# Half of the U tiles of the dense experts: 4 KB rows and PE transposes in place of 1 KB rows and DVE transposes

## The chip, the cores and the metric

The kernel runs on one core of a Trainium2 chip. The metric is the device time of one execution in microseconds; the runs shown of the kernel before took 2079.33, 2078.69 and 2074.76 us.

## What is computed

Two blocks on 512 tokens of width 1024: a pool mixer with a layer norm, then a mixer (gated convolution and RG-LRU) and a PEER layer. The change lies in PEER, where each token picks 16 of 128 x 128 = 16384 experts for each of 8 heads:

```
q = (xb @ w_q).reshape(p, PEER_HEADS, 2, PEER_DK_HALF)
sc = jnp.einsum('phcd,hcnd->phcn', q, sub_keys)
...                                     # top 16 key pairs per head: idx, softmax weights g
act  = gelu(einsum('phkd,pd->phk', expert_u[idx], xb))
out  = einsum('phk,phkd->pd', g * act, expert_v[idx])
```

`expert_u` (U) and `expert_v` (W) are 16384 x 1024 in float32.

## The kernel before

One token tile of 128 gathers its experts by index (POOL issues the indirect DMAs, DVE does a multiply with a row sum for U and a multiply-add for V). The other 384 tokens treat PEER densely: for all 16384 experts, 128 at a time ("an expert" below is such a block of 128; there are 128 of them), the scores are computed, put through gelu, multiplied by the tokens' weights (zero for experts that were not picked) and multiplied with W.

An expert i has two parts. `stage_a(i)` (line 869) brings the U block into the transposed form, splits it into `uh + ul` (float32r halves), and makes 24 score products (L138 to L140, `aux<-h2h,uh` and so on, 128x384) into a side bank of PSUM; ACT's gelu gives `gl`. `stage_v(i)` (line 922) multiplies `gl` by the weights `gt` on DVE (L931), splits the result into `wh, wl`, loads and splits the W block (`wraw`, then `whi` on ACT and `wlo` on DVE or POOL by turns), and makes 18 output products (`o<-whi,wh` and so on, 128x512) into six banks that accumulate over all experts. The loop at the end of the kernel calls `stage_a(i + 11)` and `stage_v(i)` for i = 0 to 127, with the gathers of the other token tile spread between them. The scores of the first 38 experts are made earlier, so the loop makes those of 38 to 127. Every eighth expert a 1.5 MB `gt` tile is loaded (L919).

How U gets transposed depends on a type `ty`. The loop uses type 2: `u_load` (L534) reads the block in four DMAs of 128 KB in rows of 1 KB, each into 32 partitions, and `u_turn` (L539) does 32x32 transposes on DVE from `uraw` to `ut`; ACT then copies `uh` (L112) and DVE subtracts for `ul` (L116). Ten experts before the loop use type 0: one DMA in whole rows of 4 KB (L877), eight 128x128 transposes on PE into two side banks (L881), and ACT copies out of them (L883, L887).

The raw tiles of U and W share three buffers of the tag `wraw`. All loads are issued by SP's queue in order. A scheduler orders the instructions of each engine when the kernel is built, so an engine's order is not the order of the code. In the loop two PSUM banks (`side_bank`) serve the transposes and score products.

Of the kernel before, what the change touches and what calls it, by code (L numbers as in the profile page):

```python
# [13 lines left out]
OP = mybir.AluOpType  # L14
# [10 lines left out]
NG = 1  # L25
# [53 lines left out]
def _body(tc, nc, a, outer):  # L79
# [13 lines left out]
    def banks(stack, n):  # L93
        """the banks from here on, n of them for what waits on other engines"""
        nonlocal ps, psum, naux
        psum.close()
        psum, naux = stack, n
        ps = psum.enter_context(tc.tile_pool(name="ps", bufs=1, space=PSUM, reuse_waits="tile"))
# [4 lines left out]
    def side_bank():  # L103
        """for what waits on other engines, so that it holds up no other product"""
        return ps.tile([P, 512], F32, name="aux", tag="aux", bufs=naux)

    def split(hi, lo, src, pool=False):
        """src = hi + lo exactly, each in the 12 bits that a float32r product carries"""
        if pool > 1:
            G.tensor_copy(hi, src)  # L110
        else:
            S.activation(hi, src, AF.Copy)  # L112
        if pool:
            G.tensor_tensor(lo, src, hi.bitcast(F32), op=OP.subtract)  # L114
        else:
            V.tensor_tensor(lo, src, hi.bitcast(F32), op=OP.subtract)  # L116
# [164 lines left out]
    def last_group(g, mhl, sz):  # L281
        """gates and outputs of the last group, one half of the tokens after the other"""
# [138 lines left out]
    def nrsqrt(v, scale, eps, pool=False, plus=False):  # L421
        """-1/sqrt(v*scale + eps) of one column (or its negative): an estimate, then one Newton step"""
        new = lambda nm: tiny.tile([P, 1], F32, name=nm, tag=nm)
        w, s, q, r = new("rw"), new("rs"), new("rq"), new("rr")
        S.activation(s, v, AF.Abs_reciprocal_sqrt, bias=epst[:, eps], scale=4.0 * scale)      # ~ 1/2 of the root's inverse
        (G if pool else V).tensor_scalar(w, v, 4.0 * scale, epst[:, eps], op0=OP.mult, op1=OP.add)
        if plus:
            m = new("rm")
            (G if pool else V).tensor_scalar(m, s, -1.0, None, op0=OP.mult)
        else:  # L430
            m = s
        if pool:
            G.tensor_tensor(q, s, s, op=OP.mult)
            G.tensor_tensor(q, q, w, op=OP.mult)
            G.tensor_scalar(r, q, -3.0, m, op0=OP.add, op1=OP.mult)
            return r
        V.scalar_tensor_tensor(q, s, w, s, op0=OP.mult, op1=OP.mult)
        V.scalar_tensor_tensor(r, q, -3.0, m, op0=OP.add, op1=OP.mult)
        return r

    def rms(t, xn, dve=False):
        """xn = -ya[t] / rms(ya[t])"""
        ss = tiny.tile([P, 1], F32, name="ss", tag="ss")
        S.activation(xn, ya[t], AF.Square, accum_out=ss)
        r = nrsqrt(ss, 1.0 / D, E4, NP[1])
        if dve:
            V.tensor_scalar(xn, ya[t], r, None, op0=OP.mult)
        else:
            S.activation(xn, ya[t], AF.Copy, scale=r)

    def norm_T(pool, xn, t, which, put):
        """transposes xn (tokens of tile t), modulates, and splits"""
# [18 lines left out]
    # columns of the two modulations: -g*(1+scale) and shift; the second in the order of expert products  # L471
# [59 lines left out]
    def u_load(raw, i, a0, na):  # L531
        """rows 32a+r, columns 256q+8c+k of 128 experts: partition (q, r)"""
        for q in range(4):
            nc.sync.dma_start(raw[32 * q:32 * q + 32],  # L534
                              U[i * P + a0 * 32:i * P + (a0 + na) * 32, q * 256:(q + 1) * 256].rearrange("(a r) d -> r a d", r=32))

    def u_turn(ut, raw):
        """the 32x32 transposes: partition (q, c)"""
        V.transpose(out=ut.rearrange("p k (a r) -> p a k r", r=32), in_=raw.rearrange("p a (c k) -> p a k c", k=KD))  # L539

    def pre_u(n):
        """expert tiles with the columns on the partitions, for later"""
# [15 lines left out]
    V.scalar_tensor_tensor(m4, lam, -1.0, lam, op0=OP.mult, op1=OP.min)        # -|lam|  # L558
# [3 lines left out]
    V.tensor_tensor(s4, e4, p4, op=OP.mult)                                     # s = e/(2+e)  # L562
# [7 lines left out]
    V.scalar_tensor_tensor(p4, p4, 2.0, m4, op0=OP.mult, op1=OP.add)            # softplus(-lam)  # L570
# [42 lines left out]
    def headnorm(y, dst, gname, c):  # L613
# [3 lines left out]
        def fin():  # L617
# [6 lines left out]
            V.scalar_tensor_tensor(q, q, -3.0, r, op0=OP.add, op1=OP.mult)          # -2 times the root's inverse  # L624
# [13 lines left out]
    def lru(c, br, bi, xr, ge):  # L638
# [3 lines left out]
        S.activation(r, r, AF.Tanh, scale=sp4[:, c:c + 1])              # t = tanh(-log_a / 2)  # L642
        s_, w_, q = f("s_"), f("w_"), f("q")
        V.tensor_scalar(w_, r, 1e-30, None, op0=OP.max)
        S.activation(s_, w_, AF.Abs_reciprocal_sqrt)                            # ~ 1/sqrt(t)
# [3 lines left out]
        V.tensor_tensor(s_, s_, r, op=OP.mult)                                  # -2 sqrt(t)  # L649
        S.activation(w_, r, AF.Abs_reciprocal_sqrt, bias=1.0)  # L650
        S.activation(w_, w_, AF.Square)                                         # ~ 1/(1+t)
        V.scalar_tensor_tensor(q, r, 1.0, w_, op0=OP.add, op1=OP.mult)
        V.scalar_tensor_tensor(w_, q, -2.0, w_, op0=OP.add, op1=OP.mult)        # -1/(1+t)
        V.tensor_tensor(s_, s_, w_, op=OP.mult)                                 # sqrt(1-a^2)
        V.scalar_tensor_tensor(r, r, -1.0, w_, op0=OP.add, op1=OP.mult)         # a
        V.tensor_tensor(i_, i_, xr, op=OP.mult)
        V.tensor_tensor(s_, s_, i_, op=OP.mult)                                 # u
# [35 lines left out]
    # the chunks of the product in turn, each followed by what has become ready  # L693
# [74 lines left out]
    # the tokens of the dense experts come first  # L768
# [57 lines left out]
    def qpart(w, b, j, n):  # L826
        """queries of one head for n tiles of tokens from the j-th on"""
# [41 lines left out]
    def stage_a(i):  # L869
        uh = dn.tile([P, KD, P], F32R, name="uh", tag="uh", bufs=UB)  # L870
        ul = dn.tile([P, KD, P], F32R, name="ul", tag="ul", bufs=UB)
        ty = 4 if i < NU else ATY[i % len(ATY)] if i < RT else 2
# [130 lines left out]
    def topk(t, h0, nh):  # L1003
        """the 16 best pairs of keys of heads h0..h0+nh-1, and their weights"""
# [20 lines left out]
        # ranks (a, b) of each pick, and from them the keys  # L1025
# [63 lines left out]
    def onehot2(sT, t0):  # L1089
        """[i2 = j] of 8 tokens"""  # L1090
# [12 lines left out]
    def ahead(n):  # L1103
        """the one-hots of the n-th 8 tokens"""
# [79 lines left out]
    def paced(i):  # L1184
        """not before the products of GL experts back"""
        if len(pace) > GL >= 0:
            tc.add_manual_dep(i.ins, pace[-1 - GL].ins.name, order)
# [52 lines left out]
    for t in range(NT):  # L1240
        # the columns in parts, the last ones short
# [52 lines left out]
```

## Time and profile before

| | |
|---|---|
| runs | 2074.76, 2078.69, 2079.33 us, median 2078.69 |
| span of the profiled execution | 2087.4 us, 8.7 above that median; no other time of this execution is listed |
| the loop's steady part | 1200 to 2000 us of the span |
| busiest engines over the span | PE 88%, DVE 88% |

The span is the time from the first to the last instruction of one profiled execution; durations and waits below come from it. "Busy" of PE counts overlapping matmuls once, so the pitch from one start to the next is the better measure of its work.

### The profile page before, as it was taken

How to read it: one execution, taken by the hardware profiler on the slowest of the kernel's cores; microseconds unless marked ns; L12 is line 12 of the kernel's file. 1: busy time of each engine (PE TensorE's matmuls, PEld its weight loads, DVE VectorE, ACT ScalarE, POOL GpSimd, SP SyncE). 2: the span in 40 equal slices, each digit the busy share in tenths (PEclk: the TensorE clock that was granted, in tenths of full speed). 3: DMA queues.
4: the chain of work that ended last, by engine and by line, in shares of the span. 5: the costliest groups of instructions: out<-in, count | busy, mean ns of one | idle time of the engine just before them, and what ended most of it. 6: DMA issues, size and time to landing. Idle time of an engine off the chain costs nothing.

```text
span 2087.4 us, 26487 instructions
## 1 busy us (share of the span) xinstructions
PE 1832.4 (88%) x8939; PEld 1588.0 (76%) x8939; DVE 1844.1 (88%) x3005; ACT 812.8 (39%) x1162; POOL 939.1 (45%) x599
## 2 busy tenths in 40 slices
PE   8999898878899868788989898898988988898897
PEld 6787677756698857788867787787877877787796
DVE  8999887889759999999799998898988988989956
ACT  4433333445353345778432232232232232322334
POOL 3113222342453565442356555464555545556524
PEclk9999999989999978999999999999999999999999
DMA  5545482666352324444959999999989999999932
GB/s 166 178 141 179 141 284 74 185 203 195 118 167 80 114 80 135 152 168 183 311 184 283 300 291 272 272 265 277 298 262 278 296 270 277 294 270 293 289 124 101
DMA packets 291748, 441.11 MB, mean 211 GB/s; under 512 B 24984, under 2 KB 208132, under 8 KB 288540
## 3 DMA queue, kind: packets, MB, share of 16 engines
q1 hardware_dynamic: 254748, 305.19, 48.8%
q0 software_dynamic: 36864, 134.23, 20.7%
q8 instruction: 70, 1.15, 0.2%
q14 instruction: 66, 0.54, 0.1%
HBM read 393.11 MB, written 46.23 MB: 210 GB/s over the span
## 4 chain that ended last, share of the span: by engine, by line
DVE 38%; DMA 23%; PE 15%; issue 13%; POOL 5%; SPq 2%; ACT 2%; DVEq 0%; POOLq 0%; ACTq 0%
DMA uraw<-in_expert_u 8%; DVE og L1132 8%; DMA wraw<-in_expert_v 4%; DMA gv<-in_expert_v,idx 4%; PE bank L140 3%; PE bank L139 3%; PE bank L138 3%; DVE ut L539 3%; DMA araw<-in_w_ada 2%; DVE wlo L116 2%; SPq L534 2%; POOL wlo L114 2%; DVE sw L239 2%; DVE put L539 2%; DMA praw<-in_expert_u 1%
## 5 line engine op out<-in xcount | busy, mean ns | idle before, releaser
L114 POOL TENSOR_TENSOR wlo<-wraw,whi 128x1024 fp32r<-128x1024 f32 x116 | 304.0, 2621 | 465.2 <-ACT whi L112 438.9
L140 PE MATMUL aux<-h2h,ul 128*128 128x384 f32 x1024 | 369.2, 361 | 90.2 <-DVE ul L116 78.4
L112 ACT ACTIVATE whi<-wraw 128x1024 fp32r<-128x1024 f32 x218 | 229.5, 1056 | 509.8 <-DMA wraw<-in_expert_v 375.6
L138 PE MATMUL aux<-h2h,uh 128*128 128x384 f32 x1024 | 365.1, 357 | 16.8 <-ACT uh L112 9.8
L139 PE MATMUL aux<-h2l,uh 128*128 128x384 f32 x1024 | 360.4, 352 | 0.0
L139 PE MATMUL o<-wlo,wh 128*128 128x512 f32 x756 | 298.0, 394 | 17.5 <-DVE wlo L116 12.6
L140 PE MATMUL o<-whi,wl 128*128 128x512 f32 x756 | 293.9, 392 | 0.2 <-DVE wl L116 0.2
L138 PE MATMUL o<-whi,wh 128*128 128x512 f32 x756 | 292.3, 393 | 1.4 <-ACT wh L112 1.4
L140 PEld LDWEIGHTS aux<-h2h,ul 128*128 128x128 f32 x1024 | 203.5, 199 | 110.0 <-DVE ul L116 95.9
L1180 POOL DMA_INDIRECT gv<-in_expert_v,idx x128 | 188.0, 1469 | 206.3 <-DVE acc L1203 170.1
L539 DVE STREAM_TRANSPOSE ut<-uraw 128x1024 f32<-128x1024 f32 x98 | 213.7, 2182 | 66.1 <-DMA uraw<-in_expert_u 65.6
L1180 POOL DMA_INDIRECT gu<-in_expert_u,idx x128 | 173.7, 1357 | 144.1 <-DVE junk L1192 113.8
L138 PEld LDWEIGHTS aux<-h2h,uh 128*128 128x128 f32 x1024 | 204.6, 200 | 24.8 <-ACT uh L112 12.7
L139 PEld LDWEIGHTS aux<-h2l,uh 128*128 128x128 f32 x1024 | 203.7, 199 | 3.1
L1203 DVE SCALAR_TENSOR_TENSOR acc<-gv,cf,acc 128x1024 f32<-128x1024 f32 x127 | 182.5, 1437 | 9.5 <-DMA gv<-in_expert_v,idx 9.1
L112 ACT ACTIVATE uh<-ut 128x1024 fp32r<-128x1024 f32 x98 | 103.4, 1056 | 217.9 <-DVE ut L539 208.2
L139 PEld LDWEIGHTS o<-wlo,wh 128*128 128x128 f32 x756 | 143.1, 189 | 48.4 <-DVE wlo L116 15.1
L1192 DVE SCALAR_TENSOR_TENSOR junk<-gu,hrow 128x1024 bf16<-128x1024 f32 x128 | 164.1, 1282 | 12.7 <-DMA gu<-in_expert_u,idx 12.5
L1132 DVE TENSOR_SCALAR og<-iorow,sT 128x128 f32<-128x128 f32 x384 | 173.4, 521 | 0.0
L140 PEld LDWEIGHTS o<-whi,wl 128*128 128x128 f32 x756 | 143.2, 189 | 31.0 <-DVE wl L116 0.6
L138 PEld LDWEIGHTS o<-whi,wh 128*128 128x128 f32 x756 | 142.9, 189 | 28.9 <-ACT wh L112 1.7
L1134 PE MATMUL bank<-og,o 128*128 128x128 f32 x768 | 119.2, 302 | 48.6 <-DVE og L1132 47.1
(379 smaller groups left out, 3754.3 us busy)
## 6 DMA issues: line engine op xcount, KB each, us to landing
wraw<-in_expert_v SPq DMA_DIRECT2D x128, 512.0 KB
uraw<-in_expert_u SPq DMA_DIRECT2D x392, 128.0 KB
araw<-in_w_ada SPq DMA_DIRECT2D x96, 256.0 KB
g_d<-gs SPq DMA_DIRECT2D x24, 1024.0 KB
gt<-g_d SPq DMA_DIRECT2D x15, 1536.0 KB
wraw<-in_pool_w_in SPq DMA_DIRECT2D x32, 512.0 KB
wraw<-in_w_in SPq DMA_DIRECT2D x20, 512.0 KB
praw<-in_expert_u SPq DMA_DIRECT2D x160, 64.0 KB
```

Source lines behind the costliest of these rows:

```text
L112: S.activation(hi, src, AF.Copy)
L114: G.tensor_tensor(lo, src, hi.bitcast(F32), op=OP.subtract)
L116: V.tensor_tensor(lo, src, hi.bitcast(F32), op=OP.subtract)
L138: i = PE.matmul(out, lhsT=l[0], rhs=r[0], start=first, stop=False)
L139: PE.matmul(out, lhsT=l[0], rhs=r[1], start=False, stop=False)
L140: PE.matmul(out, lhsT=l[1], rhs=r[0], start=False, stop=last)
L539: V.transpose(out=ut.rearrange("p k (a r) -> p a k r", r=32), in_=raw.rearrange("p a (c k) -> p a k c", k=KD))
L1132: V.tensor_scalar(og, iorow, sT[:, 0, tok + u:tok + u + 1], sT[:, 2, tok + u:tok + u + 1], op0=OP.is_equal, op1=OP.mult)
L1134: PE.matmul(b[:, u * P:(u + 1) * P], lhsT=o2[:, tok % 8 + u], rhs=og, start=True, stop=True)
L1180: G.indirect_dma_start(out=r, out_offset=None, in_=src, in_offset=bass.IndirectOffsetOnAxis(ap=idx[t][:, s:s + 1], axis=0))
L1192: paced(V.scalar_tensor_tensor(junk, r, 1.0, hrow[t], op0=OP.mult, op1=OP.mult, accum_out=cf[t][:, s:s + 1]))
L1203: paced(V.scalar_tensor_tensor(acc[t], r, cf[t][:, s:s + 1], acc[t], op0=OP.mult, op1=OP.add))
```

## The change

The type of the experts past 38 becomes 2 for even and 1 for odd ones. All other differences between the two files are comments.

```
-        ty = 4 if i < NU else ATY[i % len(ATY)] if i < RT else 2
+        ty = 4 if i < NU else ATY[i % len(ATY)] if i < RT else 2 - i % 2
```

Type 1 goes through code that was there, and that no expert used. It needs no `ut` tile:

```
raw = wp.tile([P, D], F32, name="uraw", tag="wraw", bufs=3)
nc.sync.dma_start(raw, U[i * P:(i + 1) * P, :])                 # L877, one DMA
for kk in range(2):
    b = side_bank()
    for k in range(4):
        PE.transpose(b[...], raw..., ident)                      # L881
    S.activation(fl(uh), b, AF.Copy)                             # L883
    V.tensor_tensor(fl(ul), b, fl(uh).bitcast(F32), op=OP.subtract)   # L885, from PSUM
```

What the scheduler makes of it, at two places. SP's queue in the loop, with what each load waits for, before: a W load (L123) waits for DVE (the transposes that read the raw U tile in its buffer), a U load (four of L534) for the split of a W tile on POOL or DVE.

```order
L123 DMA wraw<-in_expert_v 128x1024 [waits DMAHW6_49,DMAHW7_49,DMAHW0_49,DVE_49]
L534 DMA uraw<-in_expert_u 32x4x256 [waits DMAHW1_49,Pool_49]
L534 DMA uraw<-in_expert_u 32x4x256 x2
L534 DMA uraw<-in_expert_u 32x4x256 [waits DMAHW2_49]
L123 DMA wraw<-in_expert_v 128x1024 [waits DMAHW4_49,DMAHW5_49,DMAHW3_49,DVE_49]
```

The same queue after the change, over two experts:

```order
L123 DMA wraw<-in_expert_v 128x1024 [waits DMAHW3_49,PE_49]
L534 DMA uraw<-in_expert_u 32x4x256 [waits DMAHW1_49,Pool_49]
L534 DMA uraw<-in_expert_u 32x4x256 x3
L123 DMA wraw<-in_expert_v 128x1024 [waits DMAHW3_49,DVE_49]
L877 DMA uraw<-in_expert_u 128x1024 [waits DMAHW6_49,DMAHW5_49,DMAHW7_49,DMAHW4_49,DVE_49]
```

Every second U load is one DMA (L877), and every second W load waits for PE, that is for the transposes that empty its buffer. By the semaphores' values the first W row (that of an even expert) waits for the transposes of the odd tile loaded two experts before, the second W row for the split of the first one's W on DVE, the four pieces of U for a split on POOL, and L877 for DVE's transposes of the U tile in the row before. The load of gt stands between a W load and an odd tile's L877.

PE's order in the loop before: 24 score products and 18 output products in strict turn; here the end of an expert's output products and the start of the next scores.

```order
L140 MATMUL o_9645<-whi,wl 128x512
L138 MATMUL aux<-h2h,uh 128x384
L139 MATMUL aux<-h2l,uh 128x384
L140 MATMUL aux<-h2h,ul 128x384
```

After the change: the second group of four transposes stands after six output products of an expert, and the first group in front of them. The remaining 12 follow, then the 48 score products of an odd and an even expert, most often with six output products of the next expert put among them.

```order
L138 MATMUL o_9640<-whi,wh 128x512
L139 MATMUL o_9640<-wlo,wh 128x512
L140 MATMUL o_9640<-whi,wl 128x512
L138 MATMUL o_9641<-whi,wh 128x512
L881 MATMUL aux<-ident,uraw 128x128 x4
L139 MATMUL o_9641<-wlo,wh 128x512
L140 MATMUL o_9641<-whi,wl 128x512
```

What moved: the turn on PE is now by two experts, and the transposes stand among output products.

## Rows read from the trace of the kernel before

**Rows 1.** The page's first part: busy us of each engine, its share of the span of 2087.4 us, and its instructions.
```profile
PE 1832.4 (88%) x8939; PEld 1588.0 (76%) x8939; DVE 1844.1 (88%) x3005; ACT 812.8 (39%) x1162; POOL 939.1 (45%) x599
```

**Rows 2.** Busy time by engine in the loop's steady part (columns: stretch, its length, busy us and instructions of PE, PEld, DVE, ACT, POOL; granted clock; DMA share; GB/s).
```profile
1200.00:2000.00 800.00, 709.10 (x3394) 632.05 (x3393) 717.85 (x710) 236.94 (x334) 427.75 (x269) 0.96 0.96 278
```

**Rows 3.** PE's groups of instructions from 1200 to 2000 us (busy us, mean ns of one, then idle time before them and what ended it).
```profile
L140 PE MATMUL aux<-h2h,ul 128*128 128x384 f32 x645 | 232.5, 360 | 74.1 <-DVE ul L116 74.0
L138 PE MATMUL aux<-h2h,uh 128*128 128x384 f32 x646 | 228.9, 354 | 15.1 <-ACT uh L112 8.1 <-ACT gl L904 6.9
...
L139 PE MATMUL o<-wlo,wh 128*128 128x512 f32 x486 | 189.7, 390 | 1.7 <-POOL wlo L114 1.7
L138 PE MATMUL o<-whi,wh 128*128 128x512 f32 x485 | 189.5, 391 | 0.0
L140 PE MATMUL o<-whi,wl 128*128 128x512 f32 x486 | 189.3, 390 | 0.0
```

**Rows 4.** Busy time by engine in three stretches around a load of gt (columns as in rows 2).
```profile
1304.00:1340.00 36.00, 35.13 (x179) 31.83 (x178) 36.00 (x36) 11.43 (x16) 19.80 (x13) 1.00 1.07 298
1340.00:1348.00 8.00, 3.98 (x18) 2.97 (x16) 0.01 (x1) 0.00 (x0) 0.96 (x1) 0.97 1.06 241
1348.00:1356.00 8.00, 3.98 (x11) 3.47 (x12) 7.62 (x9) 2.91 (x4) 1.89 (x2) 0.50 0.64 170
```

**Rows 5.** SP's queue and DVE in order of time in the same place (start, duration, queue, line, what; in brackets idle time and releaser).
```profile
1325.70 0.39 SPq L919 DMA_DIRECT2D gt<-g_d  x1
1327.97 9.61 SPq L534 DMA_DIRECT2D uraw<-in_expert_u  x4
...
1338.94 7.66 SPq L534 DMA_DIRECT2D uraw<-in_expert_u  x4
...
1354.36 1.73 SPq L534 DMA_DIRECT2D uraw<-in_expert_u  x4
...
1348.25 2.01 DVE L539 STREAM_TRANSPOSE ut<-uraw 128x1024 f32<-128x1024 f32 x1 [8.24 <-DMA uraw<-in_expert_u]
```

**Rows 6.** DVE's transposes in the 25 us from a load of gt on: the first (from 1248 us), the second (1325 us) and the last (1894 us) of nine such stretches; in the others the idle time is 3.8 to 5.8 us.
```profile
L539 DVE STREAM_TRANSPOSE ut<-uraw 128x1024 f32<-128x1024 f32 x2 | 4.4, 2184 | 2.0 <-DMA uraw<-in_expert_u 2.0
L539 DVE STREAM_TRANSPOSE ut<-uraw 128x1024 f32<-128x1024 f32 x2 | 4.3, 2140 | 8.2 <-DMA uraw<-in_expert_u 8.2
...
L539 DVE STREAM_TRANSPOSE ut<-uraw 128x1024 f32<-128x1024 f32 x2 | 4.3, 2136 | 2.7 <-DMA uraw<-in_expert_u 2.7
```

**Rows 7.** DVE's groups for a U tile from 1200 to 2000 us.
```profile
L539 DVE STREAM_TRANSPOSE ut<-uraw 128x1024 f32<-128x1024 f32 x83 | 181.5, 2186 | 62.8 <-DMA uraw<-in_expert_u 62.3 <-issue 0.4
L116 DVE TENSOR_TENSOR ul<-ut,uh 128x1024 fp32r<-128x1024 f32 x81 | 104.9, 1295 | 1.1 <-ACT uh L112 1.1
```

**Rows 8.** PE in order of time: the first score product of an expert, the first output product after it, and the first score product of the next.
```profile
1401.78 0.34 PE L138 MATMUL aux<-h2h,uh 128*128 128x384 f32 x1
...
1406.00 0.40 PE L138 MATMUL o<-whi,wh 128*128 128x512 f32 x1
...
1410.09 0.34 PE L138 MATMUL aux<-h2h,uh 128*128 128x384 f32 x1
```

**Rows 9.** Groups over the whole span, shapes kept apart: a subtraction on DVE with a PSUM source, ACT's copy of half a U tile out of PSUM, and of a whole one from SBUF.
```profile
L116 DVE TENSOR_TENSOR sl<-bank,sh 128x512 fp32r<-128x512 f32 x16 | 10.8, 680 | 4.3 <-ACT sh L112 4.3
L883 ACT ACTIVATE uh<-aux 128x512 fp32r<-128x512 f32 x20 | 12.4, 618 | 5.0 <-PE aux L881 5.0
L112 ACT ACTIVATE uh<-ut 128x1024 fp32r<-128x1024 f32 x98 | 103.4, 1056 | 217.9 <-DVE ut L539 208.2 <-PE aux L139 4.7 <-DVE wlo L116 2.8
```

**Rows 10.** PE in order of time around the eight transposes of a type 0 tile, and the busy time of the 4 us around it (columns as in rows 2).
```profile
995.13 1.04 PE L881 MATMUL aux<-ident,uraw 128*128 128x128 f32 x8
996.14 0.44 PE L140 MATMUL aux<-h2h,ul 128*128 128x384 f32 x1
...
994.00:998.00 4.00, 4.00 (x29) 3.84 (x28) 0.00 (x0) 4.00 (x8) 2.54 (x2) 1.00 0.87 273
```

**Rows 11.** SP's issues of whole U tiles for type 0 (count, shortest, median and longest ns, first and last start).
```profile
L877 SPq DMA_DIRECT2D uraw<-in_expert_u x10: 332/333/333, 822.4 to 959.0; - x10
```

**Rows 12.** DMA in two windows of 5 us, 1260 to 1265 (mostly 1 KB packets) and 1625 to 1630 (mostly 4 KB): packets, MB, rate, and how many packets are under each size.
```profile
DMA packets 797, 1.11 MB, mean 222 GB/s; under 512 B 90, under 2 KB 662, under 8 KB 797
...
DMA packets 507, 1.85 MB, mean 371 GB/s; under 512 B 53, under 2 KB 55, under 8 KB 507
```

**Rows 13.** A load of W: SP's issue and ACT's start on it, in order of time; then the times of the split's second half on DVE and on POOL from 1400 to 1480 us (shortest, median, longest ns).
```profile
1405.15 0.35 SPq L123 DMA_DIRECT2D wraw<-in_expert_v  x1
...
1413.20 1.06 ACT L112 ACTIVATE whi<-wraw 128x1024 fp32r<-128x1024 f32 x1 [3.92 <-DMA wraw<-in_expert_v]
...
L116 DVE TENSOR_TENSOR wlo<-wraw,whi x4: 1215/1222/1229, 1407.6 to 1468.2; 128x1024 fp32r<-128x1024 f32 x4
L114 POOL TENSOR_TENSOR wlo<-wraw,whi x4: 2404/2485/3373, 1417.6 to 1472.7; 128x1024 fp32r<-128x1024 f32 x4
```

**Rows 14.** SP's queue from 1200 to 2000 us: what it waited for (us in total, times, longest).
```profile
SPq L123 <- DVE ut L539: 138.0, 61, 5.5
SPq L534 <- DVE wlo L116: 125.8, 35, 6.3
SPq L534 <- POOL wlo L114: 108.1, 29, 8.8
```

## The prediction

> **What bounds the kernel now.** I first read the page's whole-span line: PE and DVE are both busy 88% of it [rows 1], so neither alone explains the span. The change touches only the long expert loop, so I took that stretch by itself, 1200 to 2000 us [rows 2]: PE 709, DVE 718 of 800 us, DMA share 0.96. In it the products into o were issued 485 + 486 + 486 times [rows 3]; an expert has 18 of them, so 80.9 experts passed: 9.89 us each, 79.1 us for eight. Eight is the right unit, because every eighth expert a 1.5 MB gt tile is loaded.
>
> Three views then show what the 79.1 us are. *DVE.* In 36 us without a gap, 1304 to 1340, DVE is busy 36.00 us and PE 35.13 [rows 4]: between the gt loads DVE has no free time. Its work for eight experts is 718/80.9 × 8 = 71.0 us. *The gap.* In the next 8 us DVE does nothing (0.01), and 8 us later TensorE's granted clock is 0.50, its lower level of 1.2 GHz, after PE has run dry [rows 4]. The queue rows say why [rows 5]: SP issues gt at 1325.70, then the four pieces of a U tile, whose issue alone takes 9.61 us, and DVE's transpose of it starts at 1348.25 after 8.24 us of idleness that ended with that transfer. In the nine stretches of 25 us after each gt load DVE waited so for 2.0 to 8.2 us [rows 6], 41 us together, of the 62.3 us that the stage shows for this wait [rows 7]. *PE.* The products go at fixed pitch: 24 score products took 1401.78 to 1406.00, 4.22 us, the 18 output products to 1410.09, 4.09 us [rows 8]. That is 8.31 us an expert, 66.5 for eight. PE's idle time in the stage is 74.1 + 15.1 + 1.7 = 90.9 us [rows 3], or 9.0 for eight. What is left, 79.1 − 66.5 − 9.0 = 3.6, I read as lost to the clock (mean 0.96 [rows 2], and 0.04 × 79.1 is 3.2). So PE loses 12.6 of every 79.1 us, nearly all by waiting for ul and uh, which DVE and the transfers before it bring late.
>
> **The change, part by part.** From expert 39 to 127 the odd ones change: 45 tiles, over 90 experts, or 11.25 times eight with four changed tiles each. Before that point the order of instructions is the same.
>
> *DVE.* Each changed tile loses the 32x32 transposes, 2186 ns, and the subtraction of 1295 ns [rows 7]; it gains two subtractions with a PSUM source, for which the nearest row is sl<-bank at 680 ns [rows 9]. Net −2186 − 1295 + 1360 = −2121 ns, −8.5 us for eight: DVE's work falls to 62.5 and DVE stops being the fullest engine.
>
> *ACT.* Two halves of 618 ns from PSUM replace one of 1056 [rows 9]: +0.18 us on an engine busy 237 of 800 us [rows 2]. Nothing, covered by ACT's idleness; should that cover go (ACT waits in order behind whi), it is at most 0.18 × 45 = 8 us.
>
> *PE.* Eight transposes are added. The trace has ten such tiles in an earlier stage: eight took from 995.13 to the next product at 996.14, 1.01 us [rows 10]. So +4.0 for eight experts: PE's own work is 70.5 and nothing hides it when PE has no gap. The clock was 1.00 in the 4 us around them [rows 10]. The Trainium skill, "TensorE: Matmul & The Clock Gate", Part 4, gives about 275 ns for one such transpose in a kernel (for bf16) and says that transposes do not engage the clock gate; that would be 2.2 us a tile, and the sum below would come out 1.2 × 45 = 54 us later. The trace disagrees on the first, with 126 ns each, and shows no drop.
>
> *DMA.* The bytes stay, the rows grow from 1 KB to 4 KB, and four issues become one of 0.33 us [rows 11] in place of four that took between 1.73 and 9.61 us [rows 5]. In a 5 us window full of 1 KB packets the engines moved 222 GB/s, in one of 4 KB packets 371 [rows 12]. A 0.524 MB tile is then 2.36 us of all 16 engines against 1.41, so 0 (if the neighbours in those windows make the difference) to 0.95 us less per tile, 3.8 for eight. I take it as real. By the Trainium skill, "DMA: Bandwidth & Descriptors", Specifications, rows from 512 B up already reach line rate, and the term would be 0; the two windows say otherwise, though gathers run in both.
>
> *Moved waits.* SP's order keeps its alternation, but a changed tile's buffer is now freed by PE, not DVE, and W tiles wait for that (SP's order, shown with the change). PE's order changes more: two experts' score products now stand together, and the transposes in two groups of four among the output products. A late raw tile now blocks PE directly, with both kinds of products queued behind it. On the other side the tile behind gt is always an odd one, thus one of the changed: it is one transfer, and PE takes it up only after the next two experts' products have been issued, so a late landing there can be absorbed.
>
> *The sum.* PE sets the end: 70.5 plus what PE still loses. If all 12.6 stay, eight experts take 83.1, +4.0 × 11.25 = +45 us. If all go, 70.5, −8.6 × 11.25 = −97 us. Break-even is 8.6 lost. I take the odd half of the waits for uh and ul as gone: (74.0 + 8.1)/80.9 × 8 = 8.1 a group of eight, half 4.05; the clock's 3.6 falls in proportion to the 9.0 of idleness, by 1.6. Lost: 12.6 − 5.65 = 6.95; eight experts 77.4; −1.65 × 11.25 = **−18.6 us**. The profiled span of 2087.4 becomes 2069; the runs' median is 8.7 us below that span, so I forecast 2078.7 − 18.6 = **2060**.
>
> **The rivals.** *Faster by much: the gap after gt closes.* For it: the tile that DVE waits for behind gt is a changed one, and 41 of the 62.3 us of that wait lie there. If PE's loss falls to 4, eight experts take 74.5: −4.6 × 11.25 = −52 us, 2027. Against: the even tile that follows gt keeps four pieces, whose issue took 7.66 us at the same place [rows 5]. By the Trainium skill's 512 B (the same section) the tile's length would not change, and this case would fall to a third of its chance.
>
> *Slower: the raw buffers come free too late.* Three buffers carry U and W. By the built program's waits, in a pair of experts W of the even one waits for the transposes of an odd tile on PE, and W of the odd one for the split of that W: two loads in a row. From SP's issue to ACT's start a W load took 8.05 us (1405.15 to 1413.20), its split 1.06 + 1.23 on DVE or 1.06 + 2.49 on POOL [rows 13]: 10.3 + 11.6 = 21.9 us. From W's arrival PE's order needs 12.5 us to the transposes that free the buffer of the next-but-one pair (6 + 12 output products, 34 score products, 8 transposes and 6 more output products, at the pitches above). The chain spans two pairs, so a pair takes (21.9 + 12.5 + w)/2 = 17.2 + w/2, where w is waiting in SP's, ACT's, DVE's and POOL's queues; a pair now takes 19.8. It decides from w = 5.2 on. SP's waits for such buffers are long now: 138 us in 61 waits for ut, 126 in 35 for wlo on DVE, 108 in 29 on POOL [rows 14], 2 to 4 us each. With w = 9 a pair takes 21.7: +1.9 × 45 = +86, 2164. Milder, with PE's loss unchanged, it is the +45 above, 2124. Against it: loads get lighter and DVE's queue shorter.
>
> *No difference.* PE's loss falls by just the 4.0 that the transposes add: 2075 to 2083. Two runs shown agree only to 0.2%, about 4 us, which is what I count as no change.
>
> *Dearer transposes.* With the Trainium skill's 2.2 us a tile (the section on transposes above) the forecast would be 2060 + 54 = 2114; I give this 3 in 100, since the row is direct.
>
> **How the numbers follow.** My forecast (2040 to 2074) 33%, the closed gap 20%, no difference 12%, the loss unchanged or worse (2083 to 2135) 22%, the buffer chain above that 10%, dearer transposes 3%. Faster by over 0.2%: 33 + 20 = 53%; within 0.2%: 12%; slower: 22 + 10 + 3 = 35%. For the range I leave out the lower third of the closed gap and most of the buffer chain: 2005 to 2130.
>
> **What would show it.** Right: DVE's busy time in the loop about 95 us lower (45 × 2.12), no gap on DVE that ends with uraw after a gt load, PE's idle time a third to a half lower and its clock nearer 1.00, transposes at about 1 us for eight. Wrong: PE idle before the transposes or before output products with a transfer or wlo as releaser; SP's queue waiting for PE ahead of wraw; a pair of experts above 20 us; or DMA still at 0.96 with unchanged GB/s, which would say that 4 KB rows give nothing.

## The result and the profile after

The changed kernel takes **2091.53 us** (median of 20 runs, 2073.23 to 2097.61), the kernel before 2076.89 in the same sessions (20 runs, 2068.80 to 2083.63): ratio 1.0062 [1.0046, 1.0077], some 13 us slower by the ratio. The forecast was 2060, so its direction was wrong; its range held the time. The profiled execution of the changed kernel has a span of 2093.6 us against 2087.4; the one of the kernel before is longer than each of its 20 runs, so the two traces show less than the whole difference, and may show the waits before as longer than they mostly were.

Busy time from 1200 to 2000 us (columns as in [rows 2]), and that stretch's DMA in total, which for the kernel before was 120308 packets, 80094 of them under 2 KB (the same view), at a share of 0.96 [rows 2]:

```profile
1200.00:2000.00 800.00, 737.69 (x3700) 658.98 (x3699) 653.53 (x700) 241.46 (x369) 389.34 (x265) 0.97 0.85 274
...
DMA packets 101701, 219.34 MB, mean 274 GB/s; under 512 B 8352, under 2 KB 56966, under 8 KB 101651
```

DVE's busy time fell from 718 to 654 us, the DMA share from 0.96 to 0.85 with nearly the same bytes, and PE is busier by 29 us. Yet no more experts pass. PE's groups of the same stretch, which answer [rows 3] (busy us, mean ns, idle time before and what ended it):

```profile
L138 PE MATMUL aux<-h2h,uh 128*128 128x384 f32 x641 | 224.3, 350 | 39.2 <-DVE ul L885 34.2 <-ACT uh L883 4.5
L140 PE MATMUL aux<-h2h,ul 128*128 128x384 f32 x641 | 221.9, 346 | 9.3 <-DVE ul L885 9.3
...
L139 PE MATMUL o<-wlo,wh 128*128 128x512 f32 x485 | 192.3, 397 | 1.7 <-POOL wlo L114 1.6
...
L138 PE MATMUL o<-whi,wh 128*128 128x512 f32 x486 | 173.7, 410 | 3.9 <-ACT whi L112 3.9
L881 PE MATMUL aux<-ident,uraw 128*128 128x128 f32 x320 | 48.3, 277 | 8.2 <-ACT gl L904 8.1
```

485 output products of a kind passed, as before: 80.9 experts. PE's idle time is 62.3 us instead of 90.9. The waits of [rows 3] for ul from line 116 and uh from line 112 have gone altogether, for even tiles too. In their place stand waits for the changed tiles' own halves, 34.2 + 9.3 us for DVE at line 885 and 4.5 for ACT at line 883, and 8.1 us in which the transposes wait for a side bank that a gelu has not read yet. With as many experts in the same 800 us, eight still take 79.1 us, so PE loses 79.1 − 70.5 = 8.6, the prediction's break-even: 6.2 of it idle, and the other 2.4 I put down to the clock (0.97).

DVE's groups, which answer [rows 7], and the longest waits of ACT and DVE (us in total, times, longest):

```profile
L539 DVE STREAM_TRANSPOSE ut<-uraw 128x1024 f32<-128x1024 f32 x40 | 87.3, 2183 | 37.9 <-DMA uraw<-in_expert_u 37.9
L116 DVE TENSOR_TENSOR ul<-ut,uh 128x1024 fp32r<-128x1024 f32 x41 | 66.5, 1621 | 0.1
L931 DVE TENSOR_TENSOR gl<-gl,gt 128x384 f32<-128x384 f32 x80 | 60.4, 755 | 34.8 <-ACT gl L904 34.8
...
L885 DVE TENSOR_TENSOR ul<-aux,uh 128x512 fp32r<-128x512 f32 x79 | 53.7, 683 | 0.0
L116 DVE TENSOR_TENSOR wlo<-wraw,whi 128x1024 fp32r<-128x1024 f32 x41 | 50.0, 1220 | 49.3 <-ACT whi L112 49.3
```

```profile
ACT whi L112 <- DMA wraw<-in_expert_v: 213.8, 49, 11.2
ACT gl L904 <- PE aux L140: 175.7, 52, 11.9
...
DVE wlo L116 <- ACT whi L112: 49.3, 19, 5.8
```

The changed tiles' durations are those forecast: 683 ns for a half out of PSUM (680 in [rows 9]), 2183 for the transposes. An even tile's subtraction grew from 1295 ns [rows 7] to 1621, for a reason that no run here shows; that is a part of why DVE's busy time fell by 64 us and not by the 85 that 40 tiles at 2.12 make. DVE gave back its time as 84 us of waiting for ACT.

One turn shows the new wait. These rows are in order of time, first DVE's, then ACT's, then PE's (start, duration, what; in brackets idle time and its end; "..." stands for rows left out):

```profile
1328.89 0.54 DVE L931 TENSOR_TENSOR gl<-gl,gt 128x384 f32<-128x384 f32 x1
1330.86 1.23 DVE L1192 SCALAR_TENSOR_TENSOR junk<-gu,hrow 128x1024 bf16<-128x1024 f32 x1 [1.43 <-DMA gu<-in_expert_u,idx]
...
1333.25 1.28 DVE L1203 SCALAR_TENSOR_TENSOR acc<-gv,cf,acc 128x1024 f32<-128x1024 f32 x1 [1.16 <-DMA gv<-in_expert_v,idx]
1334.46 0.55 DVE L116 TENSOR_TENSOR wl<-gl,wh 128x384 fp32r<-128x384 f32 x1
1334.92 0.68 DVE L885 TENSOR_TENSOR ul<-aux,uh 128x512 fp32r<-128x512 f32 x1
1335.53 3.79 DVE L116 TENSOR_TENSOR ul<-ut,uh 128x1024 fp32r<-128x1024 f32 x1
```

```profile
1328.46 0.60 ACT L883 ACTIVATE uh<-aux 128x512 fp32r<-128x512 f32 x1
```

```profile
1327.82 0.60 PE L881 MATMUL aux<-ident,uraw 128*128 128x128 f32 x4
...
1332.63 0.39 PE L140 MATMUL o<-whi,wl 128*128 128x512 f32 x1
1335.66 0.45 PE L138 MATMUL aux<-h2h,uh 128*128 128x384 f32 x1 [2.64 <-DVE ul L885]
1335.95 0.34 PE L139 MATMUL aux<-h2l,uh 128*128 128x384 f32 x1
1336.13 0.34 PE L140 MATMUL aux<-h2h,ul 128*128 128x384 f32 x1
```

ACT had copied the first half at 1329.06. DVE subtracts it only at 1334.92, behind two gather sums for which it first sat idle 1.43 and 1.16 us, and PE, out of output products, stands 2.64 us. The product at 1335.66 reads uh, not ul; what it waits for is one of the two side banks, which the half held from 1327.82 on. But the bank alone cost little. These are the odd tile's products (the even tile's ul, line 116, is written only from 1335.53 to 1339.32), and the third of them, 0.47 us later, reads the very ul that this subtraction writes. A free bank would have let two products pass. What PE waited for is the late subtraction, and the same holds of the other waits of L138 for line 885: in each the product that reads ul follows within 0.5 to 0.8 us.

The gain and the loss lie at different ends. PE's idle time went from 62.2 to 31.2 us between 1200 and 1700 us, from 15.1 to 16.2 between 1700 and 1850, from 9.2 to 12.6 between 1850 and 1950. Over the latter two stretches the DMA share is 0.78 and 0.79 after, 0.97 before. There an in-order ACT is late, here in the changed kernel (all engines in order of time):

```profile
1885.29 1.06 ACT L112 ACTIVATE whi<-wraw 128x1024 fp32r<-128x1024 f32 x1 [11.15 <-DMA wraw<-in_expert_v]
...
1886.25 0.47 ACT L904 ACTIVATE gl<-aux 128x384 f32<-128x384 f32 x1
...
1886.78 1.11 PE L881 MATMUL aux<-ident,uraw 128*128 128x128 f32 x4 [2.73 <-ACT gl L904]
...
1888.86 0.33 SPq L123 DMA_DIRECT2D wraw<-in_expert_v  x1
```

ACT waits 11.15 us for a W tile; the gelu behind it in ACT's order keeps a side bank, the transposes wait for that bank, and the next W is issued 3.6 us after the first was taken up.

### The profile page after: what moved, and what is told of

Read it like the earlier page. It is cut to its first block, busy times and chain, and to the rows that moved or that the text cites. A ratio compares the mean times of both kernels' runs of the same rounds, so it can differ in the third digit from the quotient of the medians.

```text
span 2093.6 us, 26933 instructions
## 1 busy us (share of the span) xinstructions
PE 1864.3 (89%) x9299; PEld 1619.3 (77%) x9299; DVE 1780.5 (85%) x3005; ACT 822.6 (39%) x1207; POOL 904.1 (43%) x599
## 4 chain that ended last, share of the span: by engine, by line
DVE 38%; DMA 22%; PE 18%; issue 11%; POOL 7%; ACT 3%; SPq 2%; DVEq 0%; POOLq 0%; ACTq 0%
DVE og L1132 8%; DMA gu<-in_expert_u,idx 6%; DMA wraw<-in_expert_v 6%; POOL wlo L114 4%; DMA uraw<-in_expert_u 3%; PE bank L139 2%; PE bank L140 2%; PE bank L138 2%; DVE ut L539 2%; DVE wlo L116 2%; DMA araw<-in_w_ada 2%; DMA praw<-in_expert_u 2%; PE aux L138 2%; PE aux L140 2%; DVE sw L239 2%
## 5 line engine op out<-in xcount | busy, mean ns | idle before, releaser
L138 PE MATMUL aux<-h2h,uh 128*128 128x384 f32 x1024 | 362.3, 354 | 43.5 <-DVE ul L885 37.9
L140 PE MATMUL aux<-h2h,ul 128*128 128x384 f32 x1024 | 360.0, 352 | 23.3 <-POOL ul L894 11.5
L140 PE MATMUL o<-whi,wl 128*128 128x512 f32 x756 | 297.3, 396 | 0.2 <-DVE wl L116 0.2
L138 PE MATMUL o<-whi,wh 128*128 128x512 f32 x756 | 274.5, 405 | 5.8 <-ACT whi L112 4.1
L138 PEld LDWEIGHTS aux<-h2h,uh 128*128 128x128 f32 x1024 | 200.9, 196 | 58.1 <-DVE ul L885 49.6
L1180 POOL DMA_INDIRECT gv<-in_expert_v,idx x128 | 160.2, 1252 | 180.9 <-DVE acc L1203 158.1
L1180 POOL DMA_INDIRECT gu<-in_expert_u,idx x128 | 163.3, 1276 | 149.0 <-DVE junk L1192 111.1
L140 PEld LDWEIGHTS aux<-h2h,ul 128*128 128x128 f32 x1024 | 200.1, 195 | 32.3 <-DVE ul L885 16.2
L116 DVE TENSOR_TENSOR wlo<-wraw,whi 128x1024 fp32r<-128x1024 f32 x102 | 132.1, 1296 | 69.1 <-ACT whi L112 69.0
L1192 DVE SCALAR_TENSOR_TENSOR junk<-gu,hrow 128x1024 bf16<-128x1024 f32 x128 | 172.7, 1349 | 16.7 <-DMA gu<-in_expert_u,idx 16.4
L138 PEld LDWEIGHTS o<-whi,wh 128*128 128x128 f32 x756 | 144.6, 193 | 33.3 <-ACT whi L112 6.1
L140 PEld LDWEIGHTS o<-whi,wl 128*128 128x128 f32 x756 | 143.8, 190 | 28.7 <-DVE wl L116 0.6
L1134 PEld LDWEIGHTS bank<-og,o 128*128 128x128 f32 x768 | 108.7, 209 | 57.5 <-DVE og L1132 28.2
```

Source lines behind the costliest of these rows:

```text
L138: i = PE.matmul(out, lhsT=l[0], rhs=r[0], start=first, stop=False)
L140: PE.matmul(out, lhsT=l[1], rhs=r[0], start=False, stop=last)
L1134: PE.matmul(b[:, u * P:(u + 1) * P], lhsT=o2[:, tok % 8 + u], rhs=og, start=True, stop=True)
L1180: G.indirect_dma_start(out=r, out_offset=None, in_=src, in_offset=bass.IndirectOffsetOnAxis(ap=idx[t][:, s:s + 1], axis=0))
L1192: paced(V.scalar_tensor_tensor(junk, r, 1.0, hrow[t], op0=OP.mult, op1=OP.mult, accum_out=cf[t][:, s:s + 1]))
```

## The experiments

Where the expectations name theories: A is that PE's own work for the transposes decides, B that raw buffers come free too late, C that the lighter loads (rows) do; later R and D are about DVE's relief, P and S about the side banks. Ratios are to the kernel before; microseconds in the text are ratio times 2078. The diffs are cut to the lines that matter; those of rows4k_dve, rows4k_none, rows4k_four, rows1k_spread, unread and before_4buf are against the kernel before, the others against the changed one. The scheduler orders each version anew, so a difference of two runs holds the new order as well.

**rows4k_dve**: the rows without the transposes on PE. Odd tiles come by one DMA of 4 KB rows and are turned on DVE as before (the elements of these tiles then stand in another order).

```diff
+ if i >= RT and i % 2:
+     nc.sync.dma_start(raw.rearrange("p a d -> p (a d)"), U[i * P:(i + 1) * P, :])
+ else:
      u_load(raw, i, 0, 4)
```


> The odd tiles are loaded by one DMA in 4 KB rows but still transposed by DVE (the tile's elements then stand in the wrong order, so their scores are not the reference's); no transposes on PE. Theory C (the rows are the useful half of the change, the PE transposes the harmful one): the DMA share falls, the waits of DVE for uraw shrink by half, 15 to 30 us faster than before, about 2055. Theory A (PE's own work decides; DVE was relieved for nothing) says the rows alone leave DVE full as before: within 6 us of before, 2071 to 2083. Theory B (late raw buffers) has no PE release here, so at most 5 us from A.

Measured 2041.75 us, ratio 0.9824 [0.9799, 0.9850]: 37 us faster than before, more than theory C had (15 to 30); A and B fall. The first row is its steady part, the second a wait in it:

```profile
1200.00:2000.00 800.00, 739.71 (x3590) 662.72 (x3589) 732.95 (x725) 250.04 (x350) 419.68 (x270) 0.98 0.87 282
...
DVE ut L539 <- DMA uraw<-in_expert_u: 18.1, 7, 5.2
```

DVE does as much per tile as before and yet PE gains: DVE's wait for raw tiles fell from 62.3 us [rows 7] to 18.1. Much of DVE's lateness thus came from the loads and not from its own work.

**rows1k_pe**: the transposes on PE without the rows. Odd tiles keep four DMAs in pieces of 1 KB and are turned on PE (elements in another order).

```diff
- nc.sync.dma_start(raw, U[i * P:(i + 1) * P, :])
+ u_load(raw.rearrange("p (a d) -> p a d", a=4), i, 0, 4)
```


> The odd tiles are loaded by four DMAs in 1 KB rows as before, but transposed on PE (again in the wrong order of elements). Theory C: all of the cost and none of the gain, 15 us or more above the changed kernel, 2106 and up. Theory A: PE's work is that of the changed kernel, so within 6 us of it, 2086 to 2098. Theory B: the same as A or somewhat later, since each load in the chain lasts longer: 2092 to 2105.

Measured 2146.03 us, 1.0332 [1.0313, 1.0352]: +69 us, as theory C had it. Moving the transposes to PE, DVE's relief included, costs 69 us at 1 KB rows and 50 at 4 KB (from 0.9824 to 1.0062).

**twice**: each transpose of the changed kernel's odd tiles is done two times.

```diff
+ for _ in range(2 if ty else 1):
      PE.transpose(...)
```


> The changed kernel with each of its PE transposes of odd tiles done twice (16 per tile; the result is the reference's). Theory A: PE sets the pace, so the added 45 x 1.0 us shows nearly whole, +35 to +45 on the changed kernel, 2127 to 2137. Theory B: PE has idle time that takes it up, under +15, below 2107.

Measured 2130.15 us, 1.0259 [1.0234, 1.0283]: +41 us on the change, 0.91 us for eight, as theory A had it. The price of 1.01 us [rows 10] was nearly right, and PE hides little or nothing of it. "TensorE: Matmul & The Clock Gate", Part 4, of the Trainium skill has about 275 ns for one transpose in a kernel, for bf16. A row above has 277 as the mean duration too (f32), but they overlap, and the second eight cost 114 ns each here.

**odd_to_95**: the change only for odd experts below 96.

```diff
- 2 - i % 2
+ 2 - i % 2 if i < 96 else 2
```


> The change for the odd experts 39 to 95 only (29 tiles), type 2 after. Theory B (the gain made in the first two thirds is lost in the last third, where W loads wait one for another): keeps the lead that the changed kernel's trace has at two thirds, 10 to 18 us faster than before, 2059 to 2067. Theory A: cost in proportion to the tiles, 29/45 of the +14, so about +9, 2086.

Measured 2062.63 us, 0.9943 [0.9921, 0.9965], as theory B had it: 12 us faster than before, 25 faster than the full change. The 29 earlier tiles gain, the 16 last ones lose 1.5 us each. From 1700 to 1850 its DMA share is 0.96, against 0.78 with the full change.

**behind_gt**: PE turns only the tiles with i % 8 = 3, 11 in all, meant to be those right behind gt. In this run's trace that is so for experts 43, 51 and 59 alone; from 67 on the tile is issued ahead of gt, and the one behind gt (68, 76 and so on) is even and has its four pieces.

```diff
- 2 - i % 2
+ 1 if i % 8 == 3 else 2
```


> Only every eighth expert (43, 51, ..., 123: 11 tiles) is of type 1, the odd one whose load follows that of gt in the queue. The transposes add 11 us to PE. If the tile behind gt is what DVE waits for (the gap of the forecast), the gap halves: 41 us of waits for uraw after gt become 20 or less, and the kernel is 5 to 12 us faster than before, about 2068. Theory A without that: +11 at most, within 2076 to 2088.

Measured 2098.18 us, 1.0083 [1.0056, 1.0110]: +17 us, a miss for both expectations, and no test of the gap behind gt. PE's two longest waits from 1200 to 2000 us:

```profile
PE aux L881 <- ACT gl L904: 27.0, 5, 7.2
PE o L139 <- POOL wlo L114: 23.5, 6, 7.8
```

Five waits of the transposes for a side bank cost 27 us: with few such tiles a late gelu still blocks PE whole. Another 23.5 us went to late splits of W on POOL, 1.7 before [rows 3].

**all_pe**: all tiles from expert 38 on by the changed way.

```diff
- 2 - i % 2
+ 1
```


> All experts from 38 on are of type 1 (90 tiles). Theory A: PE's own work for eight experts is 74.5 us, DVE's 54: the added 45 us are not paid by anything, since the waits of the odd tiles had gone already: +30 to +45 on the changed kernel, 2120 to 2137. Theory B (the mixture of two kinds of tile in three buffers makes the chain): one kind of tile again, no chain, and DMA lighter by as much again: under +15, 2075 to 2105.

Measured 2181.42 us, 1.0475 [1.0449, 1.0502]: 90 us on the change, later than both theories had it (A 2137 at most). DVE is busy 527 of 800 us and the DMA share is 0.76, so neither is full. SP's longest waits are those of rival "buffers" for PE:

```profile
SPq L123 <- PE aux L881: 171.3, 36, 9.7
SPq L877 <- PE aux L881: 129.0, 23, 11.8
```

PE's own longest wait is now for W:

```profile
PE o L138 <- ACT whi L112: 57.2, 22, 5.8
```

With every tile turned on PE the loads wait for PE and PE waits for the loads: the chain of that rival, in a version that theory B had expected to be free of it.

**after_4buf** and **before_4buf**: a fourth raw buffer in the changed kernel and in the one before (the space is taken from the ring of tiles og, 11 in place of 16).

```diff
- nraw, nbuf = 3, 3
+ nraw, nbuf = 4, 3
```


> The changed kernel with four raw buffers in place of three (and 11 instead of 16 og buffers in the stage before, to make room). Theory B: the chain of W loads goes, 15 to 30 us faster than the changed kernel, 2061 to 2076. Theory A: PE's work is the same, within 8 us of the changed kernel, 2083 to 2099.

> The kernel before with four raw buffers and 11 og buffers, the control of the run with four. DVE is full between the gt loads, so a fourth buffer helps only in the gaps: 0 to 12 us faster than before, 2065 to 2077. If the buffers bound the kernel before as well, 20 us faster or more.

Measured 2099.23 us, 1.0087 [1.0056, 1.0118], no faster than the change (the upper end of theory A's range), and 2063.81 us, 0.9916 [0.9892, 0.9939], 17 us faster than before, between the two expectations. So a fourth raw buffer helps the kernel before but not the changed one: as a cause of the loss that rival falls.

**rows4k_none**: odd tiles in 4 KB rows, split as they lie, turned by nobody (their products are of untransposed data).

```diff
+ nc.sync.dma_start(raw.rearrange("p a d -> p (a d)"), U[i * P:(i + 1) * P, :])
+ split(uh, ul, raw.rearrange("p a (k d) -> p (a k) d", k=2), ty == 3)
```


> From expert 38 on the odd tiles come by one DMA of 4 KB rows and are split as they lie, turned by nobody (their products are of untransposed data); even tiles as before. It stands between the kernel with 4 KB rows and DVE transposes (2041.75) and the changed kernel (2091.53): DVE is relieved as in the change, PE gets no added work. Theory R (the lighter loads are all that was gained; DVE's relief is worth next to nothing since its idle time turns into waits for ACT): 2036 to 2044, which makes the PE transposes cost some 50 us. Theory D (DVE's relief counts, as the prediction's 8.5 us per eight experts says; in 11 octets some 40 us at most for half of the waits): 2000 to 2025, which would make the PE transposes cost 65 to 90 us.

Measured 2023.10 us, 0.9733 [0.9700, 0.9765]: 19 us less than with DVE's transposes. Theory R falls, and D's range (2000 to 2025) holds the time at its upper end: relief of DVE is worth something, but about half of the 40 us that D gave as its most. It makes the whole cost of the transposes on PE 68 us (from 0.9733 to 1.0062).

**dve_kept**: the change, and DVE turns the odd tiles as well, for nobody.

```diff
+ u_turn(ut, raw.rearrange("p (a d) -> p a d", a=4))
```


> The changed kernel, in which DVE does the 32x32 transposes of the odd tiles as well, into a tile that nobody reads: the change without DVE's relief (some 45 tiles by 2.18 us = 98 us of DVE back). Theory R (relief is worth next to nothing): 2085 to 2100, as the changed kernel's 2091.53, give or take the odd tile's raw buffer that comes free a little later. Theory D (relief counts): 2110 to 2140.

Measured 2117.05 us, 1.0188 [1.0155, 1.0221]: +26 us on the change for 45 × 2.18 = 98 us of DVE's work. Theory R falls here too, and D's range holds it; DVE's time counts by about a quarter, with the raw buffer's later release in that figure.

**rows4k_four** and **rows1k_spread**: what makes the load light. Four DMAs of 32 whole rows into 32 partitions each (another order of elements); and four DMAs in 1 KB pieces, each of 32 whole experts over all 128 partitions (the same tile as before). DVE turns both.

```diff
+ for j in range(4):
+     nc.sync.dma_start(raw[32 * j:32 * j + 32].rearrange("p a d -> p (a d)"), U[i * P + 32 * j:i * P + 32 * j + 32, :])
```
```diff
+ for j in range(4):
+     nc.sync.dma_start(raw[:, j], U[i * P + 32 * j:i * P + 32 * j + 32, :].rearrange("r (q d) -> q r d", q=4))
```


> Odd tiles from expert 38 on by four DMAs, each of 32 whole 4 KB rows into 32 partitions, turned on DVE as before (the order of the elements in the tile is another, so products of these tiles are of mixed-up data). Same bytes and same number of DMAs as before; only the row length differs from the kernel before. If the row length is what makes the load light: within 6 us of 2042 (one DMA, 4 KB rows, DVE). If it is the number of DMAs that SP issues and waits for: within 6 us of 2077.

> Odd tiles from expert 38 on by four DMAs in pieces of 1 KB, but each DMA takes 32 whole experts and spreads their four quarters over all 128 partitions, where before each took one quarter of all 128 experts into 32 partitions; turned on DVE, the same result. If pieces of 1 KB are the cost, or four DMAs are: 2070 to 2080, as before. If the load is slow because each DMA goes to 32 partitions alone, or reads DRAM in pieces 4 KB apart: 2040 to 2050.

Measured 2064.53 us, 0.9922 [0.9893, 0.9951], and 2213.15 us, 1.0644 [1.0611, 1.0677]. Of the 37 us that the rows give, 16 come with the row length alone and some 20 with one DMA in place of four (and into all 128 partitions in place of 32 each); both expectations lay to either side. The spread pieces were expected at 2040 to 2050 or 2070 to 2080 and cost 134 us more than before; DVE's wait for raw tiles, first with four DMAs of rows, then spread:

```profile
  DMA uraw<-in_expert_u: 38.2, 17
```
```profile
  DMA uraw<-in_expert_u: 140.1, 32
```

"DMA: Bandwidth & Descriptors", Specifications, of the Trainium skill has line rate from 512 B on; by it four DMAs of 4 KB rows would cost the same as four of 1 KB pieces. The run disagrees, by 16 us.

The spread load does not test the piece length. In the traces each of its DMAs posts 5 arrivals on its semaphore, where each of the four-piece loads in the kernel before and in rows4k_four posts 16; the last arrival comes 8.9 us after the end of the issue at the median (180 DMAs), against 4.3 for the four-piece loads of the kernel before (552). That looks as if each spread DMA ran in fewer parallel parts. Whether the partitions or these parts made it slow, no run separates.

**unread**: as rows4k_none, and PE transposes the odd tiles into the side banks for nobody.

```diff
+ for kk in range(2):
+     b = side_bank()
+     for k in range(4):
+         PE.transpose(b[:, k * P:(k + 1) * P], ..., ident)
  split(uh, ul, raw..., ty == 3)
```


> As the kernel whose odd tiles are turned by nobody (2023.1: 4 KB rows, split as they lie), but PE does the eight transposes of each odd tile into the side banks, and nobody reads them (the products of odd tiles are of untransposed data). PE has all the work of the change, the side banks need no emptying. Theory P (the transposes cost their own time on PE and no more; the rest of the 68 us is bad luck elsewhere): the changed kernel's time, 2085 to 2095. Theory S (PE's own 45 us, plus 23 us because each half of a tile holds one of two side banks until DVE's subtraction, in its order behind the gather sums, has read it): 2060 to 2075.

Measured 2077.68 us, 0.9988 [0.9968, 1.0009]: 53 us on rows4k_none, 15 below the change. PE's transposes and score products in it:

```profile
L138 PE MATMUL aux<-h2h,uh 128*128 128x384 f32 x650 | 223.1, 343 | 0.3 <-ACT uh L112 0.3
L140 PE MATMUL aux<-h2h,ul 128*128 128x384 f32 x650 | 223.0, 343 | 21.6 <-DVE ul L116 21.6
...
L902 PE MATMUL aux<-ident,uraw 128*128 128x128 f32 x328 | 49.6, 285 | 32.2 <-ACT gl L912 32.2
```

The 39.2 us of idle time ahead of L138 have gone with the emptying; but L140 waits 21.6 us for late subtractions, and the transposes 32.2 us, not 8.2, for banks that gelus hold. The time lies 3 us above theory S's range and 7 below P's: reading the transposes back costs 15 us, not the 23 of S. This difference holds the late subtraction and the held bank together. The 53 us exceed the transposes' own 41 to 45; PE's idle time from 1200 to 2000 us rose too, from 40.0 us in rows4k_none to 57.4.

**early_free**: the changed kernel, but ACT copies each half out of its bank twice, and DVE subtracts once from SBUF.

```diff
- V.tensor_tensor(fl(ul), b, fl(uh).bitcast(F32), op=OP.subtract)
+ S.activation(fl(ut), b, AF.Copy)
+ if kk:
+     V.tensor_tensor(ul, ut, uh.bitcast(F32), op=OP.subtract)
```


> The changed kernel, with the side banks emptied by ACT alone: ACT copies each half to SBUF a second time (two more copies of about 0.6 us a tile), and DVE subtracts once, 1.3 us, from SBUF. Same work for PE, the same for DVE, 1.2 us a tile more for ACT, which is idle over half of the time. Theory S: the waits of PE for DVE's ul before a score product (34.2 and 9.3 us in 800) go, 2065 to 2080, if ACT's own waits for W tiles don't hold the banks as long. Theory P: no difference, 2088 to 2095, or later by up to 10 where ACT's queue is late.

Measured 2127.77 us, 1.0234 [1.0203, 1.0266]: 36 us slower than the change and outside both ranges, so the cure that theory S proposed fails.

```profile
L138 PE MATMUL aux<-h2h,uh 128*128 128x384 f32 x613 | 218.9, 357 | 32.5 <-ACT ut L885 29.1 <-ACT uh L112 3.3
...
L140 PE MATMUL aux<-h2h,ul 128*128 128x384 f32 x613 | 212.1, 355 | 19.1 <-DVE ul L887 19.0
...
L138 PE MATMUL o<-whi,wh 128*128 128x512 f32 x468 | 162.0, 411 | 21.5 <-ACT whi L112 21.4
```

The wait for a bank is nearly as long, now behind ACT (ut 29.1), which sits 231.9 of 800 us waiting for W tiles with this work queued behind them; and the output products now wait 21.4 us for ACT as well. The cure also makes ul later, since DVE subtracts only when both halves are copied (19.0 us at L140); so this run can't tell a held bank from a late ul.

**odd95_4buf**: the two edits with a gain together.

```diff
- nraw, nbuf = 3, 3
+ nraw, nbuf = 4, 3
- 2 - i % 2
+ 2 - i % 2 if i < 96 else 2
```


> The change for odd experts below 96 only, and a fourth raw buffer: the two edits with a gain together, and the result is that of the reference. If the gains (13 us and 15 us) are of different waits: 2045 to 2053. If the fourth buffer gives only what the lighter tiles give already, or as with the changed kernel (2091.5 to 2099.2) nothing: 2060 to 2070.

Measured 2064.16 us, 0.9929 [0.9907, 0.9951]: the gains don't add, as the second expectation had it. That both take the same waits for late loads is a guess. Three versions that compute the whole result beat both kernels by about as much: odd_to_95, before_4buf and this one.

## Why the prediction was wrong, point by point

Taken apart by the runs, the 13 us (with a few us of uncertainty in each term, and the terms in this order of steps) are

| step | from, to | us |
|---|---|---|
| 4 KB rows by one DMA | before, rows4k_dve | −37 |
| DVE rid of its transposes of odd tiles | rows4k_dve, rows4k_none | −19 |
| the transposes' place on PE | rows4k_none, unread | +53 |
| reading the transposes back out of the side banks | unread, after | +15 |

**The step that failed** is the sum's account of PE: it took "the odd half of the waits for uh and ul as gone", 12.6 − 5.65, and set against it only the +4.0 of the transposes, with nothing for what an odd tile waits for on its new way. The sum thus had +45 and −64; the runs show +68 and −56, so 23 of the 31 us by which it erred lie in the cost and 8 in the saving. The new way leads from PE to ACT to DVE and back to PE, through two side banks that the score products need as well, with both readers in order behind late W tiles and gather sums. "Moved waits" said that PE could absorb a late raw tile, but put no price on a late reader. The old waits went for odd and even tiles alike, a larger saving than I took, and the new ones, 48 us for the odd tiles' own halves and 8 for banks in 800, stood in their place. The Trainium skill says beside its figure for a transpose ("TensorE: Matmul & The Clock Gate", Part 4) that its output lands in PSUM and needs a copy from there; I had costed that copy by its duration on DVE and ACT, and not by when it comes round. The runs agree that it costs: 15 us. No run gave the transposes more lead or a third bank, so how much of this a held bank adds to the late subtraction stays open; in the turn shown the late subtraction is most of the wait.

**DVE as the fullest engine: half right.** DVE was full between gt loads, as [rows 4] shows, but full is not the same as in the way. Relief of some 95 us was worth 19 to 26. The larger part of the saving, 37 us, came from the rows, the term that I called real (0.95 us a tile, 43 for 45 tiles) and then left out of the sum since PE sets the end. That its size comes near is partly luck: some 20 of the 37 us came with one DMA in place of four, not with the row length that I had worked it out from. PE was late because DVE was late, and DVE in large part because of the loads.

**PE's price: nearly right.** 0.91 us for the second eight in twice, where the forecast had 1.01. **Even lost time: wrong.** I spread 12.6 us evenly over 11.25 groups of eight. The saving came in the first two thirds alone; odd_to_95 shows that the last 16 odd tiles only cost, 25 us. Why the loads thin out so much there (DMA share 0.78) I could not settle: with a fourth raw buffer it is 0.86 from 1700 to 1850 us, and the time is no shorter. SP's issues wait for W tiles' splits on POOL and DVE, which wait for ACT; no run changed that order.

**The tile behind gt** is odd up to expert 99, but even for 108 and 116, and so not always odd as I said; the wait for uraw fell from 62.3 to 37.9 us, not to none. So the closed gap came in part and was not enough; behind_gt, meant to test it, did not.

**The rivals.** "The loss unchanged", 2124, and "no difference" bracket the result: the loss fell to the break-even in the steady part, and the end added the rest. The buffer chain is in the traces (SP waits 171 us for PE in all_pe), but in the changed kernel SP's waits for PE's transposes come to 27 us in 800, and a fourth buffer gives nothing. Dearer transposes are excluded by twice: at 2.2 us for eight it would have cost 99 us and not 41. Of the signs I named, DVE's fall (64 us in 800, three quarters of the forecast) and PE's idle time (a third lower) came much as for a right forecast. So did the DMA share. None of them tells the end; the signs that did, score products waiting for line 885 and transposes waiting with a bank's reader as the releaser, were not on my list.

## What to carry to other kernels

In this kernel a step moved to the engine that sets the end cost its own time in full, plus the time until in-order readers, busy with late work of others, had brought its result back and freed its buffer: follow the result through its readers' queues, and do not count their microseconds alone. Where an engine is full and late, try the lighter load alone before moving its work: here the load gave 37 us and the relief 19. And ask of each saving in which part of the run the waits that it removes really lie.

## What the runs showed of the hardware that was not expected

The same 512 KB in four DMAs of 1 KB pieces took the kernel from 2079 to 2213 us when each DMA took its pieces from 32 whole rows into 128 partitions, in place of one quarter of 128 rows into 32. An issue of one then took 562 ns at the median, against 432 for the even tiles' in the same run, each posted 5 arrivals on its semaphore in place of 16, and DVE waited 140.1 us for the tiles. With whole rows, four DMAs of 32 partitions in place of one of 128 cost some 20 us of the kernel's time, bytes and row length being equal.
